# A one-core block with a 16-expert mixture: down ahead of gate and up at the last two lists, and the last list's small operations behind the row tiles

## Chip, cores and metric

The kernel runs on one core of a Trainium2 chip. The metric is the device time of one execution in microseconds (us); where several runs are named it is their median. Engines: PE multiplies matrices, DVE and ACT work elementwise, POOL does small operations and the indirect transfers, SP issues most of the plain transfers. Each engine runs its own instructions in the order in which they were written into its queue.

## The reference, cut to what matters

```python
def hier_moe(h, lp):                       # h: 512 tokens x 1024
    ...                                    # router: one group of 4, then the top 2 of its 4 experts
    y = jnp.zeros_like(h)
    for e in range(N_EXPERTS):             # 16 experts, 1024 -> 512 -> 1024
        a = jax.nn.silu(h @ lp['w_gate'][e]) * (h @ lp['w_up'][e])
        y = y + combine[..., e, None] * (a @ lp['w_down'][e])
    return y

x = x + gate1 * rmsnorm(token_mix(...), g_post_mix)
h2 = modulate(rmsnorm(x, g_pre_ffn), shift2, scale2)
x = x + gate2 * rmsnorm(hier_moe(h2, lp), g_post_ffn)
```

The parts ahead of `hier_moe` are the same in both kernels, and the change touches only what comes last.

## The kernel before

Tokens are sorted into one list per expert. The lists are worked off one after the other in the order of `SEQ`; a place in this order is a *position* n = 0 to 15, written by `position` (L1616). At each position the weights of one expert stream in from HBM: 8 loads of 512 KB for gate and up, 4 for down, issued by SP (L1305) into a ring of 25 buffers. For a full list (`heavy`, up to 128 tokens) every weight is split by ACT (L1327) and DVE (L1328) into two parts and each product is three matmuls. The short lists (`light`, 64 or 32 tokens) multiply in plain fp32 in column strips of the array. Position 13 is heavy, position 14 has 64 rows, position 15, the last, 32. Below, "list 14" is the list of position 14.

`gate_up` (L1439) multiplies by gate and up and calls hooks `mid[part]` behind each quarter; for a light list ACT then copies the sum out of PSUM (L1486). `turn_a` (L1493) transposes that (tile `at`, L1500), for a light list takes silu (ACT, L1504) and the product (DVE, L1505). `down` (L1514) multiplies by down (tiles `y0`, `y1` heavy, `yl` light), scales by the routing weight on ACT (L1555, or L1558 and L1559), and hands the rows to `release`, which POOL adds to the DRAM buffer `ybuf` with an indirect transfer (L1579, the *scatter*). Before the change, the down of position n-1 stands behind the gate and up of position n; at positions 14 and 15 it stands in the hook behind the second quarter.

The ending takes row tiles of 128 tokens. `setup` (L1819), called at position 15, issues the last weight loads, then loads of the gains (`G2`, and `G2p` for the last list), the four row tiles of x1 (`x1d`, L1830), all on SP, and on POOL an indirect gather of the last list's rows of `ybuf` (`yg`, L1838) and the four row tiles of `ybuf` (`ys`, L1841). The loads from `ybuf` can only start when the scatter of list 14 has landed. `scale(tt)` (L1848) is a square with a row sum on ACT (L1850), a scalar step on DVE (L1845), two small steps on POOL (L1846, L1855) and a product on DVE (L1852); `write(tt)` (L1857) is one DVE operation (L1859) and the store to the output (SP, L1860). The last list is not added to `ybuf`: its `yl` stays in PSUM, is added to the gathered rows (DVE, L1873), normed on its own (L1874 to L1881) and added to the output by an indirect transfer on POOL (L1887), which waits for all four stores. The order of these on each engine is that in which L1871 to L1889 are written, since `after` (L1146) ties each to the one before it on its engine.

Of the kernel before, what the change touches and what calls it, by code (L numbers as in the profile page):

```python
# [25 lines left out]
NE, DE = 16, 512  # L26
# [144 lines left out]
def bc(ap, shape):  # L171
    return ap.to_broadcast(shape)
# [5 lines left out]
def body(ctx, tc, I, C, out, dbg=None):  # L178
# [30 lines left out]
    def mm(o, l, r, start, stop):  # L209
        PE.matmul(out=o, lhsT=l, rhs=r, start=start, stop=stop)  # L210
# [92 lines left out]
    for i, nm in enumerate(("w_q", "w_k", "w_v")):  # L303
        G.dma_start(out=wst[:, 16 * i:16 * i + 16].rearrange("p (h o) -> p h o", h=4),
                    in_=I[nm].rearrange("l (h b) i o -> (l b i) h o", h=4))
    wifs = FA.get(192, "wifs")
    for i, nm in enumerate(("w_if_fwd", "w_if_bwd")):
        G.dma_start(out=wifs[:, 96 * i:96 * i + 96].rearrange("p (k j) -> p k j", k=12),
                    in_=I[nm].rearrange("l (k p) j -> p (l k) j", p=128))
# [275 lines left out]
    ybuf = dr.tile([T, D], F32, name="ybuf")  # L585
# [362 lines left out]
    for i, dst in enumerate((sh2c, s2c)):  # L948
        tp = pF("adc")
        n = 64 if i else 128  # L950
# [195 lines left out]
    def after(eng, f):  # L1146
        if eng in line and nc.cur_bb is block:
            with tc.issue_after(line[eng].ins):
                line[eng] = f()
        else:  # L1150
            line[eng] = f()
# [447 lines left out]
    def turned():  # L1599
        c, xe = fq.pop(0)  # L1600
        g = groups_of(c)
        if g > 1:
            run["nl"] += 1
            x = turn_light(xe, xtb[:, 512 * (run["nl"] % 2):512 * (run["nl"] % 2) + 512], g)
        else:
            run["nh"] += 1
            x = turn(xe, run["nh"] % 2)
        fetch_to(run["upto"])
        return x
# [6 lines left out]
    def position(n, wsrc):  # L1616
        c = SEQ[n]
        tiles = [lists_of(i) for i in ([c, NE] if c == STAR else [c])]
        pend, box = run["pend"], {}
        run["pos"] = n  # L1620
        mid = [None, None, None]
        fetch_to(run["upto"])
        if pend is not None:
            mid[0] = lambda: box.update(ya=turn_a(pend))
        if n == NE - 1:
            mid[1:] = [lambda: down(pend, box["ya"]), run["setup"]]
        xs = box["xs"] = []
        run["last"] = n == NE - 1
        ahead = lambda: xs.append(turned())
        if n + 1 < NE:  # L1630
            mid[1] = ahead
        if n == NE - 2:
            mid[1] = lambda: (ahead(), down(pend, box["ya"]))
        s_ = gate_up(tiles, wsrc, run["xs"], mid)
        if pend is not None and n < NE - 2:
            down(pend, box["ya"], mid=ahead if SEQ[n + 1] == STAR else None)
        run["pend"], run["xs"] = s_, xs
# [175 lines left out]
    fin = {}  # L1813
# [5 lines left out]
    def setup(part):  # L1819
        wsrc = run.get("wsrc")  # L1820
        if part:
            for kind, q in ((0, 3), (1, 3), (2, 0), (2, 1), (2, 2), (2, 3)):
                early[kind, q] = load(wsrc, kind, q)
                rawb.pop()
        g2 = next_raw()
        SP.dma_start(out=g2.ap, in_=bc(g2d[:, :], [128, 1024]))
        fin.update(G2=g2.ap, junk=next_raw(), ys=[next_raw() for _ in range(4)])
        fin["x1"] = [next_raw() for _ in range(4)]
        for tt in range(4):
            SP.dma_start(out=fin["x1"][tt].ap, in_=x1d[tt * 128:(tt + 1) * 128, :])  # L1830
        eng = G if part else SP
        if part:
            lb = next_raw()
            fin.update(yg=lb[:, 0:LC], G2p=lb[:, LC:2 * LC], lj=lb[:, 2 * LC:3 * LC])
            for j in range(lg_):
                m = 128 // lg_
                SP.dma_start(out=fin["G2p"][j * m:j * m + m], in_=bc(g2d[:, j * LC:j * LC + LC], [m, LC]))
            line[G] = G.indirect_dma_start(out=fin["yg"], out_offset=None, in_=parts(ybuf[:, :]), in_offset=bass.IndirectOffsetOnAxis(ap=li, axis=0),  # L1838
                                           bounds_check=T * lg_ - 1, oob_is_err=False)
        for tt in range(4):  # L1840
            line[eng] = eng.dma_start(out=fin["ys"][tt].ap, in_=ybuf[tt * 128:(tt + 1) * 128, :])  # L1841

    def inv(c):

# [25 lines left out]

    yg, lj = fin["yg"], fin["lj"]  # L1871
    sq_, tot = st[:, 24:25], psX.tile([128, 512], F32, name="tot", tag="X")
    after(V, lambda: V.scalar_tensor_tensor(yg, py, lw2, yg, op0=OP.mult, op1=OP.add))  # L1873
    after(S, lambda: S.activation(lj, yg, AF.Square, accum_out=sq_))  # L1874
    mm(tot[:, 0:1], f4, sq_, True, True)
    after(V, lambda: V.tensor_tensor(yg, yg, fin["G2p"], op=OP.mult))
    after(V, lambda: V.tensor_scalar(st[:, 26:27], tot[:, 0:1], 1.0 / D, EPS, op0=OP.mult, op1=OP.add))
    after(G, lambda: G.tensor_tensor(st[:, 25:26], st[:, 26:27], mhalf[:, 0:1], op=OP.pow))
    for tt in range(2):
        scale(tt, True)  # L1880
    after(V, lambda: V.tensor_scalar(yg, yg, st[:, 25:26], None, op0=OP.mult))  # L1881
    write(0)
    for tt in range(2, 4):
        scale(tt, True)
        write(tt - 1)
    write(3)
    after(G, lambda: G.indirect_dma_start(out=parts(outv), out_offset=bass.IndirectOffsetOnAxis(ap=li, axis=0), in_=yg, in_offset=None,  # L1887
                                          bounds_check=T * lg_ - 1, oob_is_err=False, compute_op=OP.add))
    after(S, lambda: S.mul(yob[0][:, 0:LC], py, lw2))  # L1889
# [46 lines left out]
```

## Time and profile before

| | |
|---|---|
| median of 3 runs | 633.11 us (631.62 to 636.21) |
| the profiled execution, its own time | 636.78 us |
| its span in the trace | 635.0 us |
| PE busy | 537.8 us (85%) |
| DVE, ACT, POOL busy | 352.9, 281.4, 218.8 us |
| moved by DMA | 169.27 MB, mean 267 GB/s |
| granted TensorE clock, mean | 0.94 |

The span runs from the first to the last record of the trace; 1.78 us of the execution's own time lie around it. All times below are counted from the span's start. A granted clock of 1.00 is 2.4 GHz, of 0.50 1.2 GHz.

### The profile page before, as it was taken

Reading aid. Unit: us, or ns where it says so; the run is one execution under the profiler, and the core shown is the slowest. Engines: PE = TensorE matmul, PEld = TensorE weight load, DVE = VectorE, ACT = ScalarE, POOL = GpSimd, SP = SyncE. Lnnn points to the kernel's source line nnn. Section 1 sums busy time; section 2 is a strip of 40 time slices with the busy share of each in tenths; the row PEclk is TensorE's granted clock in tenths of the full one; section 3 lists DMA queues with packets and bytes.
Section 4 is the critical chain, followed back from the end, with each engine's and each line's share of the span. In section 5 each row is a group of like instructions: output and inputs, shape, how many; then the busy total and the mean of one; then the engine's idle time right before and its main releaser. Section 6 shows DMA issues by size and latency. Waiting matters only on the chain. (4 is left out here: it accounts for less than half of the span.)

```text
span 635.0 us, 9192 instructions
## 1 busy us (share of the span) xinstructions
PE 537.8 (85%) x3097; PEld 370.3 (58%) x3097; DVE 352.9 (56%) x671; ACT 281.4 (44%) x460; POOL 218.8 (34%) x278
## 2 busy tenths in 40 slices
PE   4779989698999877999497899999999899899800
PEld 1346965587655555876286676757584545575300
DVE  3560693925336663436996989755362634673042
ACT  2560625543206243334356767546362725564130
POOL 8343850066116336816550133711312110101162
PEclk9989997899999997999798979999999999989965
DMA  9975600222399884345779799999999999999963
GB/s 265 390 265 176 257 0 6 78 62 88 110 317 290 296 345 157 118 166 199 277 263 392 253 266 392 388 344 376 398 361 386 366 389 380 382 402 389 344 223 106
DMA packets 59398, 169.27 MB, mean 267 GB/s; under 512 B 9155, under 2 KB 16835, under 8 KB 59348
## 3 DMA queue, kind: packets, MB, share of 16 engines
q1 hardware_dynamic: 51012, 156.30, 66.2%
q0 software_dynamic: 5776, 11.89, 7.2%
q10 hardware_dynamic: 2560, 0.47, 0.5%
q8 instruction: 25, 0.41, 0.3%
q14 instruction: 25, 0.20, 0.1%
HBM read 155.84 MB, written 16.73 MB: 272 GB/s over the span
## 5 line engine op out<-in xcount | busy, mean ns | idle before, releaser
L1328 DVE TENSOR_TENSOR U<-U,U 128x1024 fp32r<-128x1024 f32 x106 | 126.6, 1234 | 33.0 <-ACT U L1327 32.3
L1327 ACT CAST U<-U 128x1024 fp32r<-128x1024 f32 x106 | 107.1, 1051 | 18.1 <-PE pos L210 6.6
L210 PE MATMUL y<-U,U 128*128 128x512 f32 x352 | 93.2, 404 | 1.6 <-POOL U L213 0.6
L210 PEld LDWEIGHTS y<-U,U 128*128 128x128 f32 x352 | 64.8, 190 | 19.3 <-issue 2.0
L210 PE MATMUL gate<-U,U 128*128 128x512 f32 x166 | 50.2, 408 | 2.8 <-ACT U L1327 2.2
L210 PE MATMUL uz<-U,U 128*128 128x512 f32 x192 | 52.3, 408 | 0.2 <-ACT U L601 0.2
L210 PE MATMUL up<-U,U 128*128 128x512 f32 x164 | 49.7, 400 | 1.5 <-DVE U L1328 0.8
L213 POOL TENSOR_TENSOR U<-U,U 128x512 fp32r<-128x512 f32 (+2 forms) x32 | 42.7, 1348 | 6.5 <-ACT U L425 3.7
L210 PE MATMUL gul<-U,U 128*32 128x256 f32 (+1 forms) x368 | 44.7, 435 | 0.0
L1579 POOL DMA_INDIRECT ybuf<-U,U x8 | 13.1, 1639 | 89.6 <-ACT U L1559 63.4
L210 PEld LDWEIGHTS uz<-U,U 128*128 128x128 f32 x192 | 34.9, 189 | 11.9 <-issue 5.5
L210 PEld LDWEIGHTS gate<-U,U 128*128 128x128 f32 x166 | 31.3, 193 | 11.2 <-ACT U L1327 3.6
L1579 POOL DMA_INDIRECT ybuf<-U x8 | 14.3, 1786 | 66.4 <-ACT U L1555 38.8
L210 PEld LDWEIGHTS up<-U,U 128*128 128x128 f32 x164 | 30.9, 192 | 10.0 <-DVE U L1328 1.6
L210 PEld LDWEIGHTS gul<-U,U 128*32 128x32 f32 (+1 forms) x368 | 16.1, 116 | 18.5 <-issue 10.7
L210 PE MATMUL win<-U,U 128*128 128x512 f32 x96 | 25.6, 413 | 0.0
L1334 POOL DMA_INDIRECT U<-h2d,U x16 | 19.2, 1201 | 13.7 <-PE xlt L1346 5.5
L425 ACT CAST U<-U 128x512 fp32r<-128x512 f32 (+2 forms) x30 | 21.1, 762 | 5.7 <-DMA U<-in_w_in_dram 5.7
L213 DVE TENSOR_TENSOR U<-U,U 128x512 fp32r<-128x512 f32 (+1 forms) x18 | 15.5, 884 | 12.7 <-PE crow L210 9.0
L210 PE MATMUL yl<-U,U 128*32 128x256 f32 (+1 forms) x180 | 21.5, 438 | 0.7 <-DVE U L1505 0.7
L210 PEld LDWEIGHTS win<-U,U 128*128 128x128 f32 x96 | 18.0, 196 | 6.6 <-issue 2.5
L210 PEld LDWEIGHTS num<-U,U 128*128 128x128 f32 x128 | 17.4, 191 | 4.7 <-DVE U L920 1.7
(446 smaller groups left out, 1013.0 us busy)
## 6 DMA issues: line engine op xcount, KB each, us to landing
U<-in_w_gate_dram SPq DMA_DIRECT2D x64, 512.0 KB
U<-in_w_up_dram SPq DMA_DIRECT2D x64, 512.0 KB
U<-in_w_down_dram SPq DMA_DIRECT2D x64, 512.0 KB
U<-in_w_ada_dram SPq DMA_DIRECT2D x48, 512.0 KB
U<-in_w_in_dram SPq DMA_DIRECT2D x6, 1024.0 KB
U<-in_w_out_dram SPq DMA_DIRECT2D x4, 1024.0 KB
U<-in_x_dram SPq DMA_DIRECT2D x4, 512.0 KB
x0d<-U SPq DMA_DIRECT2D x4, 512.0 KB
```

Of the source, the lines that this page charges most:

```text
L210: PE.matmul(out=o, lhsT=l, rhs=r, start=start, stop=stop)
L213: (eng or V).tensor_tensor(o, a, b, op=OP.subtract)
L425: S.copy(hi[:, s], raw[:, s])
L1327: after(S, lambda: S.copy(hi.ap, r.ap))
L1328: after(V, lambda: V.tensor_tensor(lo.ap, r.ap, hi.ap.bitcast(F32), op=OP.subtract))
L1334: g = G.indirect_dma_start(out=xe[0:n], out_offset=None, in_=h2d[:, :], in_offset=bass.IndirectOffsetOnAxis(ap=gi[0:n], axis=0), bounds_ch ...
L1579: run["scatter"] = G.indirect_dma_start(out=to, out_offset=bass.IndirectOffsetOnAxis(ap=gi, axis=0), in_=yo[:, 0:n], in_offset=None, bound ...
```

## The change

At positions 14 and 15 the down of the list before (`turn_a` included) is called ahead of `gate_up` instead of from its hook, so its four weight loads, its matmuls and its scaling stand ahead of the gate and up of the new list. `setup` is still called behind the third quarter of position 15. In `setup` the four row tiles of `ybuf` are loaded ahead of the gather of the last list's rows. In the ending, `scale(0)` and `scale(1)` stand ahead of the last list's first operation, and its other operations stand between or behind the row tiles. Lines behind L1620 have moved by 1 to 3 in the changed file.

```diff
@@ position
-        if pend is not None:
-            mid[0] = lambda: box.update(ya=turn_a(pend))
-        if n == NE - 1:
-            mid[1:] = [lambda: down(pend, box["ya"]), run["setup"]]
         xs = box["xs"] = []
         run["last"] = n == NE - 1
         ahead = lambda: xs.append(turned())
+        if n >= NE - 2:
+
+            down(pend)
+        elif pend is not None:
+            mid[0] = lambda: box.update(ya=turn_a(pend))
         if n + 1 < NE:
             mid[1] = ahead
-        if n == NE - 2:
-            mid[1] = lambda: (ahead(), down(pend, box["ya"]))
+        else:
+            mid[2] = run["setup"]
@@ setup
+        for tt in range(4):
+            line[eng] = eng.dma_start(out=fin["ys"][tt].ap, in_=ybuf[tt * 128:(tt + 1) * 128, :])
+        if part:
             line[G] = G.indirect_dma_start(out=fin["yg"], ...)
-        for tt in range(4):
-            line[eng] = eng.dma_start(out=fin["ys"][tt].ap, in_=ybuf[tt * 128:(tt + 1) * 128, :])
@@ the ending
+    scale(0, True)
+    scale(1, True)
     after(V, lambda: V.scalar_tensor_tensor(yg, py, lw2, yg, op0=OP.mult, op1=OP.add))
+    write(0)
     after(S, lambda: S.activation(lj, yg, AF.Square, accum_out=sq_))
     mm(tot[:, 0:1], f4, sq_, True, True)
+    scale(2, True)
+    write(1)
     after(V, lambda: V.tensor_tensor(yg, yg, fin["G2p"], op=OP.mult))
     after(V, lambda: V.tensor_scalar(st[:, 26:27], tot[:, 0:1], 1.0 / D, EPS, op0=OP.mult, op1=OP.add))
+    scale(3, True)
     after(G, lambda: G.tensor_tensor(st[:, 25:26], st[:, 26:27], mhalf[:, 0:1], op=OP.pow))
-    for tt in range(2):
-        scale(tt, True)
+    write(2)
+    write(3)
     after(V, lambda: V.tensor_scalar(yg, yg, st[:, 25:26], None, op0=OP.mult))
-    write(0)
-    for tt in range(2, 4):
-        scale(tt, True)
-        write(tt - 1)
-    write(3)
```

What this does to the queues is seen at three places. The first is ACT from the scaling of list 14 (L1555) on; `gul` is the sum of gate and up of the last list, `at` its transpose, and the squares of the row tiles are the 128x1024 activations. Before:

```order
L1555 ACTIVATE U_2431<-yl,U_99 128x512
L1486 COPY U_1832<-gul 128x256
L1504 ACTIVATE U_1832<-at 128x128
L1874 ACTIVATE U_2431,U_75<-U_2431 128x256
L1850 ACTIVATE U_2431,U_75<-U_2431 128x1024
L1850 ACTIVATE U_2431,U_75<-U_2426 128x1024
L1850 ACTIVATE U_2431,U_75<-U_103 128x1024
L1850 ACTIVATE U_2431,U_75<-U_81 128x1024
```

The same stretch of ACT's queue in the changed kernel:

```order
L1555 ACTIVATE U_2431<-yl,U_99 128x512
L1852 ACTIVATE U_2431,U_75<-U_2431 128x1024
L1852 ACTIVATE U_2431,U_75<-U_2426 128x1024
L1486 COPY U_1832<-gul 128x256
L1504 ACTIVATE U_1832<-at 128x128
L1879 ACTIVATE U_2431,U_75<-U_2431 128x256
L1852 ACTIVATE U_2431,U_75<-U_103 128x1024
L1852 ACTIVATE U_2431,U_75<-U_81 128x1024
```

The squares of row tiles 0 and 1 have moved from behind the last list's operations to ahead of the copy of its `gul`; those of tiles 2 and 3 stay behind the square of its rows.

The second is PE between the transposes of list 14 and the second half of the last list's gate and up (32x256 matmuls; the 64x512 ones are the down of list 14). Before:

```order
L1500 MATMUL at<-U_81,U_1832 128x128 x4
L210 MATMUL gul<-U_2007 32x256 x2
L210 MATMUL gul<-U_2431,U_2007 32x256 x2
L210 MATMUL gul<-U_2007 32x256 x2
L210 MATMUL gul<-U_2431,U_2007 32x256 x2
L210 MATMUL gul<-U_75,U_2007 32x256 x2
L210 MATMUL gul<-U_1832,U_2007 32x256 x2
L210 MATMUL gul<-U_75,U_2007 32x256 x2
L210 MATMUL gul<-U_1832,U_2007 32x256 x2
L210 MATMUL yl<-U_2007,U_1832 64x512 x2
L210 MATMUL yl<-U_99,U_1832 64x512 x2
```

In the changed kernel:

```order
L1500 MATMUL at<-U_81,U_1832 128x128 x4
L210 MATMUL yl<-U_2007,U_1832 64x512 x2
L210 MATMUL yl<-U_2431,U_1832 64x512 x2
L210 MATMUL yl<-U_75,U_1832 64x512 x2
L210 MATMUL yl<-U_1832 64x512 x2
L210 MATMUL gul<-U_2007 32x256 x2
L210 MATMUL gul<-U_99,U_2007 32x256 x2
L210 MATMUL gul<-U_2007 32x256 x2
```

The down of list 14 has moved ahead of all of the last list's gate and up; one position earlier the heavy down of list 13 has moved ahead of all of list 14's `gul` in the same way.

The third is DVE from the last list's product (L1505) on; L1873 is the operation that adds the last `yl` to the gathered rows, L1852 the products with the gain and L1859 the sums with x1. Before:

```order
L1505 TENSOR_TENSOR U_1832<-U_1832,at 128x128
L1873 SCALAR_TENSOR_TENSOR U_2431<-yl,U_99,U_2431 128x256
L1876 TENSOR_TENSOR U_2431<-U_2431 128x256
L1877 TENSOR_SCALAR U_75<-tot 128x1
L1845 TENSOR_SCALAR U_75<-U_75 128x1
L1852 TENSOR_TENSOR U_2431<-U_2431,U_81 128x1024
L1845 TENSOR_SCALAR U_75<-U_75 128x1
L1852 TENSOR_TENSOR U_2426<-U_2426,U_81 128x1024
L1881 TENSOR_SCALAR U_2431<-U_2431,U_75 128x256
L1859 SCALAR_TENSOR_TENSOR U_2431<-U_2431,U_75,U_103 128x1024
```

In the changed kernel, where that operation is L1877, the products are L1854 and the sums L1861:

```order
L1505 TENSOR_TENSOR U_1832<-U_1832,at 128x128
L1854 TENSOR_TENSOR U_2431<-U_2431,U_81 128x1024
L1847 TENSOR_SCALAR U_75<-U_75 128x1
L1854 TENSOR_TENSOR U_2426<-U_2426,U_81 128x1024
L1877 SCALAR_TENSOR_TENSOR U_2431<-yl,U_99,U_2431 128x256
L1861 SCALAR_TENSOR_TENSOR U_2431<-U_2431,U_75,U_103 128x1024
L1847 TENSOR_SCALAR U_75<-U_75 128x1
L1854 TENSOR_TENSOR U_103<-U_103,U_81 128x1024
L1861 SCALAR_TENSOR_TENSOR U_2426<-U_2426,U_75,U_81 128x1024
L1883 TENSOR_TENSOR U_2431<-U_2431 128x256
L1884 TENSOR_SCALAR U_75<-tot 128x1
```

The products of tiles 0 and 1 have moved ahead of the operation on the last `yl`; all four sums with x1 still stand behind it.

## Rows read from the trace of the kernel before

**Rows 1.** Windows: stretch, then busy (count) per engine, granted PE clock, DMA share, GB/s

```profile
579.00:586.00 7.00, 7.00 (x29) 4.68 (x30) 3.38 (x3) 1.87 (x3) 0.00 (x0) 1.00 1.04 367
...
597.00:603.00 6.00, 3.98 (x58) 1.58 (x48) 0.29 (x1) 0.65 (x2) 1.54 (x1) 1.00 0.99 337
...
617.00:623.00 6.00, 0.00 (x0) 0.00 (x0) 5.72 (x6) 0.10 (x1) 4.24 (x4) 0.50 0.56 225
```

**Rows 2.** Timeline of POOL: start us, us, operation, [idle before, what ended it]

```profile
597.26 1.54 POOL L1579 DMA_INDIRECT ybuf<-U,U  x1 [8.48 <-ACT U L1555]
605.84 1.08 POOL L1838 DMA_INDIRECT U<-ybuf,U  x1 [7.04 <-DMA U<-g2d]
606.92 2.23 POOL L1841 DMA_DIRECT2D U<-ybuf  x4
...
626.64 1.71 POOL L1887 DMA_INDIRECT out_dram<-U,U  x1 [5.15 <-SPq L1893]
```

**Rows 3.** One line's view: issue to landing of L1579 (list 14), of L1841's first two

```profile
DMA to landing us min/median/max: 7.7/7.7/7.7
...
DMA to landing us min/median/max: 4.5/4.8/5.1
```

**Rows 4.** Timeline of DVE in the ending

```profile
610.52 0.48 DVE L1873 SCALAR_TENSOR_TENSOR U<-yl,U,U 128x256 f32<-128x256 f32 x1 [10.68 <-DMA U<-ybuf,U]
611.57 0.43 DVE L1876 TENSOR_TENSOR U<-U 128x256 f32<-128x256 f32 x1 [0.57 <-ACT U L1874]
...
612.62 0.15 DVE L1845 TENSOR_SCALAR U<-U 128x1 f32<-128x1 f32 x1 [0.24 <-ACT U L1850]
...
619.03 1.22 DVE L1852 TENSOR_TENSOR U<-U 128x1024 f32<-128x1024 f32 x1
...
621.52 1.28 DVE L1859 SCALAR_TENSOR_TENSOR U<-U,U,U 128x1024 f32<-128x1024 f32 x1
```

**Rows 5.** Timeline of PE: list 14's down, the last list

```profile
592.59 3.65 PE L210 MATMUL yl<-U,U 128*64 128x512 f32 x16
596.18 2.05 PE L210 MATMUL gul<-U,U 128*32 128x256 f32 x32
598.71 0.44 PE L1500 MATMUL at<-U,U 128*128 128x128 f32 x2 [0.47 <-ACT U L1486]
599.89 1.68 PE L210 MATMUL yl<-U,U 128*32 128x256 f32 x24 [0.75 <-DVE U L1505]
602.18 0.64 PE L210 MATMUL yl<-U 128*32 128x256 f32 x8 [0.62 <-DMA U<-in_w_down_dram]
```

**Rows 6.** Timeline of ACT in the ending

```profile
598.28 0.37 ACT L1486 COPY U<-gul 128x256 f32<-128x256 f32 x1 [1.29 <-PE gul L210]
...
611.03 0.42 ACT L1874 ACTIVATE U<-U 128x256 f32<-128x256 f32 x1 [11.52 <-DVE U L1873]
611.36 0.19 ACT L1874 ACTIVATION_READ_ACCUMULATOR U<-U 128x1 f32 x1
611.45 1.04 ACT L1850 ACTIVATE U<-U 128x1024 f32<-128x1024 f32 x1
...
612.73 1.06 ACT L1850 ACTIVATE U<-U 128x1024 f32<-128x1024 f32 x1
```

**Rows 7.** Three more windows, columns as in rows 1

```profile
555.99:559.40 3.41, 3.37 (x8) 2.69 (x9) 3.41 (x4) 3.41 (x4) 0.00 (x0) 0.50 1.03 386
...
604.00:605.00 1.00, 0.00 (x0) 0.00 (x0) 0.00 (x0) 0.00 (x0) 0.00 (x0) 1.00 0.52 190
...
607.00:608.00 1.00, 0.00 (x0) 0.00 (x0) 0.00 (x0) 0.00 (x0) 1.00 (x2) 0.59 0.40 124
```

**Rows 8.** Timeline of PE: heavy matmuls at half and at full clock

```profile
556.03 2.08 PE L210 MATMUL gate<-U,U 128*128 128x512 f32 x4 [0.53 <-DVE U L1328]
...
579.52 4.02 PE L210 MATMUL y<-U,U 128*128 128x512 f32 x17
```

**Rows 9.** Timeline of SP: down loads of list 14

```profile
573.43 4.14 SPq L1305 DMA_DIRECT2D U<-in_w_down_dram  x4
```

## The prediction

> **What bounds the kernel now.** I read the windows by stage first, then the timelines of the five engines through the last 65 us, because the chain of waits reaches back only a few microseconds from the end. The windows show two regimes [rows 1]. Up to 603 us the DMA share is 0.99 to 1.04 and PE is busy 7.00 of 7.00 us while the down of list 13 runs. From 603 us PE has nothing to do, and from 617 to 623 us DVE is busy 5.72 of 6.00 us. Between the two lies a wait for one transfer after another, and this is the stretch that the change rebuilds.
>
> The POOL timeline names that wait [rows 2, 3]. The scatter of list 14 starts at 597.26 and lands 7.7 us later, at 604.96. POOL's gather starts at 605.84, 0.88 us behind that landing; the four `ys` loads follow from 606.92, about 0.6 us apiece. The first two land 4.5 and 5.1 us after their issue, so row tile 0 is there at 611.4 and row tile 1 at 612.6. Meanwhile the last list had been finished long before: its `gul` is copied at 598.28, its `yl` begins at 599.89 and ends at 602.8 [rows 5, 6]. DVE takes it up only at 610.52, when the gather is in [rows 4]. From there the ending lasts 12.28 us on DVE: the last sum with x1 starts at 621.52 and takes 1.28 us, ending at 622.80. Store, final indirect transfer and exit follow: the trace ends 12.2 us behind that sum. In these 12.28 us nothing but DVE, ACT and the row tiles matters, and the time of the kernel moves with the end of the last sum.
>
> **The change part by part.** *Down ahead of gate and up.* No instruction is added; 24 matmuls of list 13's down and 16 of list 14's are moved, with four weight loads each past four others on SP's queue. PE is full while it happens [rows 1], so moving work within it gains little. Between list 14's transposes and its `yl` stand 16 `gul` steps today; without them `yl`, which starts at 592.59 [rows 5], starts about 0.9 us earlier. PE's switches between the two kinds of matmul become fewer, which I estimate at 0.5 us more net of the bubble that list 13's own transposes lose as cover. The scatter then starts at 595.9 instead of 597.26 and lands at 603.6. The bounds are no gain at all (PE full) and 5.0 us, the time in which SP issues four loads (4.14 us and the gap to the next) [rows 9]; I take 1.4.
>
> *Row tiles ahead of the gather.* With the same 0.88 us, the first `ys` load is issued at 604.5 instead of 606.92, the second at 605.1. The gather now stands behind them and starts near 606.9; with the 4.7 us that it took from issue to use (605.84 to 610.52) it is in at 611.6, ahead of its use below.
>
> *When row tile 1 lands.* Early bound: 605.1 plus the 5.1 us of today, 610.2. Late bound: no sooner than today, 612.6, if loads that SP issued earlier hold the DMA engines. The share is already down to 0.52 at 604 [rows 7], but tile landings grew from 4.5 to 5.1 us at that share, so at least one engine must still have been working off older loads. I take 611.6.
>
> *The squares ahead of the last list, on ACT.* This is the term that decides. ACT works in order, and the squares of row tiles 0 and 1 now stand ahead of the copy of the last list's `gul`. That copy ran at 598.28; nothing was late with it. Now it must wait for row tile 1. ACT's squares follow each other by 1.28 us (612.73 less 611.45, where tile 0's square began), so the copy starts at 611.6 + 1.28 = 612.9. From the copy to the first matmul of `yl` took 1.61 us (598.28 to 599.89) [rows 5, 6]. Behind the copy are queued the silu and all of ACT's other work; for it wait PE (transposes, `yl`), then DVE.
>
> *PE's clock.* In the ending PE's last matmul ended at 602.82, and the granted clock, 0.59 in the window 607 to 608, has fallen to half there [rows 7]. In the changed kernel PE stops about 599, behind the last `gul`, and has nothing until 613, so I take `at` and `yl` at half clock. Rows show what that means: with a granted clock of 0.50, 4 heavy matmuls took 1.88 us to the next one (0.47 each), at 1.00 17 took 4.02 us (0.24 each) [rows 7, 8]. The 32 matmuls of `yl` are of the shape that took 2.05 us for 32 [rows 5]; at half clock that is 4.1 us, and the transposes (0.44 us) and what hangs on them cost about 0.3 us more. So `yl` runs from 612.9 + 1.6 + 0.3 = 614.8 to 618.9, and DVE takes it up at 619.0, where it stood at 610.52.
>
> *What is left on DVE then.* The products of tiles 0 and 1 are done by then, hidden under `yl`. Behind the start at 619.0: 0.48; on ACT the square of the last rows, 0.42 + 0.19, then the square of tile 2 with its sum, 1.06 + 0.19, under which the first sum is hidden; then on DVE a scalar step 0.15, product 1.22, sum 1.28, the last list's 0.43 and scalar step 0.15, another 0.15, product 1.22, two sums 2.56. That is 9.5 us; DVE operations overlap by about 0.08 us at each of nine hand-overs, so 8.8 us instead of 12.28 [rows 4, 6]. The last sum ends at 627.8 instead of 622.80. The last list's final scaling comes behind it, hidden by the stores for which POOL's last transfer waits until 626.64 today [rows 2]. On SP the read of the overflow count now stands between the stores of tiles 1 and 2, which a product and a sum on DVE, 2.5 us, keep apart: no cost.
>
> Sum: 627.8 - 622.8 = **+5.0 us**. The gains, 3.5 us less on DVE and 2.4 us earlier loads, are inside this sum; the in-order wait on ACT eats more than both. Against the profiled execution's own 636.78 us this is 641.8, 0.8% more. The median of the runs shown lies 3.7 us under the profiled execution; on it the same share gives 638.1 us. One per cent, about what a measurement of this kernel can tell from no change, is 6.3 us.
>
> **The rivals.** *Row tiles land no sooner than today.* Then 612.6 replaces 611.6: +6.0 us, and up to +8 if the second half of list 14's work gains nothing and POOL's small steps wait too. For it: the share of 0.99 up to 603, and older loads still in flight. Against it: the share of 0.4 to 0.5 behind 604.
>
> *Row tiles land early, or PE's clock holds.* POOL's loads go through another queue than SP's; if an engine serves both by turns, x1's loads no longer hold them up and tile 1 lands at 610.2: +3.6 us. The Trainium skill, DMA: Bandwidth & Descriptors, section "Queues, rings and completion order", says that each DMA engine takes turns between its queues packet by packet; by that rule alone the answer would be this +3.6, and no row here shows one engine's order. With the full clock for `yl` as well it is 2.4 us less: +1.2. For the clock: nothing; PE idles longer than today.
>
> *The other side: faster.* If list 14's down really comes 5.0 us earlier, as its loads do, its scatter starts at 592.3 and lands at 600.0, tile 1 lands at 601.5 + 5.1 = 606.6, and the sum above gives 622.8, no change; with the full clock -2.4 us, and with 4.5 us to land -3.0. It decides in favour of the change from the point at which tile 1 is in before 606.6. Against it: PE full from 579 to 586, and list 14's `yl` in today's trace does not wait for its weights.
>
> *It doesn't do what it says.* List 14 comes no earlier and what ACT loses DVE gains: within 1 us of today.
>
> **How the numbers follow.** The forecast (+3.5 to +6.0 with its own bounds) gets 0.47, rows landing no sooner 0.20, rows early or clock held 0.18, faster 0.09, nothing 0.06. The predicted time is 638.1. Slower by over 1% is two thirds of the second case (0.13) and the part of the first that the spread of the runs (631.62 to 636.21) carries over 6.3 us (0.17), with 0.02 from the third: 0.32. Faster by over 1% needs the fourth case and luck: 0.03. The rest, 0.65, is within 1%. The range goes from 632.5, which leaves out most of the fourth case, to 641.5, where +8 lies.
>
> **What would show it.** Right: ACT idle for more than 10 us ahead of the square of tile 0, then two squares, then the copy of `gul`, at 611 or later; PE idle from about 599 to 613 with a granted clock of 0.50 under `yl`; DVE's operation on the last `yl` near 619, and behind it about 8.8 us to the end of the last sum. The scatter of list 14 would start near 595.9. Wrong: a copy of `gul` before 608, a `yl` of 2 us, a scatter before 594, or an ending that still takes 12 us behind the last `yl`.

## The result, and the profile after

The changed kernel takes 639.16 us (median of 15 runs, 636.54 to 641.99), the kernel before 634.01 (15 runs, 631.62 to 636.21): a ratio of 1.0084, 95% interval 1.0066 to 1.0102. It is 5.15 us slower, where +5.0 (638.1 us) was forecast.

The two profiled executions differ by only 1.7 us in span (636.7 against 635.0), because they differ ahead of the change too. The last stretch of work that stands in the same place of PE's queue in both, and in all kernels below, begins with list 12's down. Its first row in PE's timeline, in the kernel before:

```profile
568.16 2.43 PE L210 MATMUL y<-U,U 128*128 128x512 f32 x10
```

In the changed kernel the same instructions start at 564.58, so 3.58 us are added to its times when they are set beside those of before. Counted from this start, the end of the trace comes 66.84 us behind it before (635.0 - 568.16) and 72.12 after (636.7 - 564.58): +5.28 us. The end of the last sum with x1 comes 54.64 and 59.86 us behind it: +5.22.

The windows of the changed kernel, columns as in [rows 1]:

```profile
579.00:586.00 7.00, 6.29 (x31) 1.88 (x27) 0.00 (x0) 0.58 (x1) 1.54 (x1) 1.00 0.98 368
597.00:603.00 6.00, 0.00 (x0) 0.00 (x0) 0.00 (x0) 0.00 (x0) 2.27 (x4) 0.76 0.82 283
603.00:611.00 8.00, 0.46 (x2) 0.29 (x2) 0.15 (x1) 2.56 (x5) 1.85 (x3) 0.50 0.72 265
611.00:617.00 6.00, 4.10 (x35) 1.62 (x34) 3.93 (x6) 1.07 (x4) 1.65 (x2) 0.50 0.01 3
617.00:623.00 6.00, 0.36 (x2) 0.27 (x2) 5.58 (x9) 2.27 (x5) 4.33 (x4) 0.50 0.46 179
```

In the kernel before, PE was busy for 3.98 us of 597 to 603 with the end of the last list's `gul`, its transposes and its `yl` [rows 1]. That stretch is 593.4 to 599.4 here; in it PE ends `gul` at 594.88 and then has nothing. Transposes and `yl` come from 610.5 on, 4.10 us of work at a granted clock of 0.50, while the DMA engines are idle (share 0.01). They have moved behind the wait for the row tiles.

The timeline of the changed kernel, POOL, ACT, PE and DVE, answers to [rows 2, 4, 5, 6] (start us, us, operation, [idle before, what ended it]; here and below rows between those shown are left out):

```profile
564.58 2.43 PE L210 MATMUL y<-U,U 128*128 128x512 f32 x10
...
572.27 0.73 PE L210 MATMUL y<-U 128*128 128x512 f32 x2 [1.59 <-ACT U L1509]
...
587.64 2.79 PE L210 MATMUL yl<-U,U 128*64 128x512 f32 x12 [0.99 <-DVE U L1505]
...
592.30 1.54 POOL L1579 DMA_INDIRECT ybuf<-U,U  x1 [8.73 <-DMA U<-in_w_down_dram]
600.59 2.27 POOL L1840 DMA_DIRECT2D U<-ybuf  x4 [6.75 <-DMA U<-x1d]
603.16 1.08 POOL L1842 DMA_INDIRECT U<-ybuf,U  x1 [0.30 <-DMA U<-g2d]
...
607.21 1.06 ACT L1852 ACTIVATE U<-U 128x1024 f32<-128x1024 f32 x1 [15.19 <-DMA U<-ybuf]
608.39 0.15 DVE L1847 TENSOR_SCALAR U<-U 128x1 f32<-128x1 f32 x1 [20.81 <-ACT U L1852]
609.08 1.06 ACT L1852 ACTIVATE U<-U 128x1024 f32<-128x1024 f32 x1 [0.72 <-ACT U L1852]
610.14 0.35 ACT L1486 COPY U<-gul 128x256 f32<-128x256 f32 x1
610.54 0.69 PE L1500 MATMUL at<-U,U 128*128 128x128 f32 x2 [15.66 <-ACT U L1486]
611.63 0.29 DVE L1505 TENSOR_TENSOR U<-U,at 128x128 f32<-128x128 f32 x1 [3.08 <-ACT U L1504]
611.98 2.79 PE L210 MATMUL yl<-U,U 128*32 128x256 f32 x24 [0.75 <-DVE U L1505]
614.54 1.08 PE L210 MATMUL yl<-U 128*32 128x256 f32 x8
615.69 0.48 DVE L1877 SCALAR_TENSOR_TENSOR U<-yl,U,U 128x256 f32<-128x256 f32 x1 [1.44 <-PE yl L210]
...
623.16 1.28 DVE L1861 SCALAR_TENSOR_TENSOR U<-U,U,U 128x1024 f32<-128x1024 f32 x1
```

ACT waits 15.19 us for row tile 0, squares it and tile 1, and only then, at 610.14, copies the last list's `gul`, whose matmuls had ended at 594.88. PE idles for 15.66 us until the transposes. DVE's queue has the same fault: the scalar step of row tile 0 (L1847), which waits for the square, stands ahead of the last list's product (L1505). Here ACT holds the product longer, so DVE's order is not what it waits for in the end. `yl` runs from 611.98 to 615.62. From DVE's operation on it to the end of the last sum (624.44) it is 8.75 us, where [rows 4] have 12.28. The landing times of the four row tiles and of the gather:

```profile
DMA to landing us min/median/max: 6.6/8.1/9.2
...
DMA to landing us min/median/max: 8.7/8.7/8.7
```

The first two tiles took 4.5 and 5.1 us before [rows 3]; now the fastest takes 6.6.

### The profile page after: what moved, and what is told of

Read it like the earlier page. It is cut to its first block, busy times and chain, and to the rows that moved or that the text cites. A ratio compares the mean times of both kernels' runs of the same rounds, so it can differ in the third digit from the quotient of the medians.

```text
span 636.7 us, 9202 instructions
## 1 busy us (share of the span) xinstructions
PE 535.3 (84%) x3097; PEld 369.6 (58%) x3097; DVE 352.6 (55%) x671; ACT 281.5 (44%) x460; POOL 218.7 (34%) x278
## 5 line engine op out<-in xcount | busy, mean ns | idle before, releaser
L1579 POOL DMA_INDIRECT ybuf<-U,U x8 | 13.1, 1644 | 88.7 <-ACT U L1559 62.4
L210 PE MATMUL gul<-U,U 128*32 128x256 f32 (+1 forms) x372 | 43.0, 436 | 0.0
L1579 POOL DMA_INDIRECT ybuf<-U x8 | 14.5, 1808 | 65.6 <-ACT U L1555 38.8
L1500 PE MATMUL at<-U,U 128*128 128x128 f32 x58 | 10.8, 290 | 17.6 <-ACT U L1486 17.6
```

Of the source, the lines that this page charges most:

```text
L1500: PE.transpose(tp[:, q * 128:(q + 1) * 128], sg[:, q * 128:(q + 1) * 128], ident)
L1579: run["scatter"] = G.indirect_dma_start(out=to, out_offset=bass.IndirectOffsetOnAxis(ap=gi, axis=0), in_=yo[:, 0:n], in_offset=None, bound ...
```

## The experiments

All are measured beside the kernel before. "Last sum" is the end of the last sum with x1, counted from the start of list 12's down in the profiled execution, as above, with its difference to the 54.64 us of before; it is the finer measure, since a run's time moves by several us for reasons that lie ahead of this mark. The ratio is taken over the runs and isn't the quotient of the two medians.

Each "last sum" comes from one execution. Up to the scatter of list 14 it repeats well: the scatter starts 29.10 us behind the mark in the three kernels with the down in its old place (before, 2 and 7), and 27.72 to 27.76 in the change and in 1, 3, 5 and 8 to 12. Behind it the transfers differ: from the scatter to the issue of the first row tile it is 8.15 to 8.91 us in the change and in 3, 8 and 9, whose loads are alike up to there. A difference below some 0.8 us between two executions therefore shows little by itself.

| experiment | median, us | before, us | ratio, 95% interval | last sum |
|---|---|---|---|---|
| the change | 639.16 | 634.01 | 1.0084 (1.0066 to 1.0102) | 59.86, +5.22 |
| 1 down ahead alone | 635.45 | 634.95 | 1.0016 (0.9993 to 1.0039) | 54.27, -0.37 |
| 2 ending alone | 636.71 | 634.95 | 1.0034 (1.0013 to 1.0054) | 56.55, +1.91 |
| 3 squares behind the silu | 635.12 | 634.95 | 1.0001 (0.9976 to 1.0025) | 56.41, +1.77 |
| 4 clock kept, spread | 644.54 | 634.95 | 1.0148 (1.0114 to 1.0181) | 65.40, +10.76 |
| 5 as 3, x1 late | 635.27 | 634.69 | 0.9997 (0.9966 to 1.0028) | 54.37, -0.27 |
| 6 as 1, x1 late | 636.14 | 634.69 | 1.0012 (0.9983 to 1.0041) | 56.31, +1.67, of it 1.6 by PE's clock |
| 7 before, x1 late | 636.10 | 634.69 | 1.0033 (1.0002 to 1.0063) | 55.88, +1.24 |
| 8 clock kept, in order | 639.25 | 634.69 | 1.0070 (1.0041 to 1.0098) | 59.77, +5.13 |
| 9 clock kept longer | 638.84 | 634.40 | 1.0078 (1.0052 to 1.0104) | 58.83, +4.19 |
| 10 as 1, half of x1 late | 633.05 | 634.40 | 0.9980 (0.9950 to 1.0011) | 53.45, -1.19 |
| 11 as 3, mixed, half late | 632.92 | 634.40 | 0.9981 (0.9956 to 1.0006) | 52.75, -1.89 |
| 12 as 11, last list last | 630.17 | 634.92 | 0.9935 (0.9910 to 0.9959) | 52.14, -2.50 |

**Experiment 1: down ahead alone.** The changed kernel with `setup` and the ending of before.

```diff
@@ setup
-        for tt in range(4):
-            line[eng] = eng.dma_start(out=fin["ys"][tt].ap, in_=ybuf[tt * 128:(tt + 1) * 128, :])
-        if part:
             line[G] = G.indirect_dma_start(out=fin["yg"], out_offset=None, in_=parts(ybuf[:, :]),
...
+        for tt in range(4):
+            line[eng] = eng.dma_start(out=fin["ys"][tt].ap, in_=ybuf[tt * 128:(tt + 1) * 128, :])
@@ the ending
-    scale(0, True)
-    scale(1, True)
     after(V, lambda: V.scalar_tensor_tensor(yg, py, lw2, yg, op0=OP.mult, op1=OP.add))
...
```

> Only the position's part of the change (down ahead of gate and up at positions 14 and 15); the setup and the ending stand as in the kernel before. Against the kernel before (634.0 us). My theory: list 14's scatter starts 1.4 us earlier, measured from the start of the heavy down that both kernels share, and if the loads from the row buffer follow it, all behind it does too: 632.6 us, -1.4. If older loads hold the row tiles, so that they land no sooner, 634.0, no change. Rival (the loss sits here: bubbles on PE at positions 14 and 15): +3 us or more, 637 or later.

Its POOL and DVE timeline (list 12's down starts at 566.60, so 1.56 us are added):

```profile
594.34 1.54 POOL L1579 DMA_INDIRECT ybuf<-U,U  x1 [8.74 <-DMA U<-g2d]
603.36 1.08 POOL L1839 DMA_INDIRECT U<-ybuf,U  x1 [7.47 <-DMA U<-x1d]
...
608.55 0.48 DVE L1874 SCALAR_TENSOR_TENSOR U<-yl,U,U 128x256 f32<-128x256 f32 x1 [10.01 <-DMA U<-ybuf,U]
```

The scatter is 1.36 us earlier than in [rows 2] (595.90 against 597.26), the gather 0.92, and DVE's start only 0.41 (610.11 against 610.52). The gather took 5.2 us from issue to use instead of 4.7. So the step does what it says on PE, and the transfers behind it give most of it back: 0.37 us are left at the last sum, less than executions differ by, and in the runs nothing that can be told from zero. The case "no change" holds; the rival that the loss sits here falls.

**Experiment 2: ending alone.** The other half: `position` as in the kernel before.

```diff
@@ position
...
+        if n == NE - 1:
+            mid[1:] = [lambda: down(pend, box["ya"]), run["setup"]]
...
-        if n >= NE - 2:
-            down(pend)
...
```

> Only the setup's and the ending's part of the change; the down stands in its hooks as in the kernel before. My theory: ACT's copy of the last list's sum waits for the square of row tile 1, as in the changed kernel, and without the earlier scatter the loss is the changed kernel's 5.2 us and 1.4 more: 640.6 us; if older loads hold the row tiles anyway, 639.2, as late as the changed kernel. Rival (the loss sits in the positions): 634 to 636. In its trace the copy would stand behind two squares and the last yl would take 3.6 us at a granted clock of 0.50.

It fell between the two, and the trace shows that the expectation rested on a wrong queue. ACT's timeline:

```profile
593.96 0.37 ACT L1486 COPY U<-gul 128x256 f32<-128x256 f32 x1 [1.85 <-PE gul L210]
...
606.93 1.06 ACT L1851 ACTIVATE U<-U 128x1024 f32<-128x1024 f32 x1 [11.73 <-DMA U<-ybuf]
```

The copy stands ahead of the squares. `after` ties the squares to each other, but nothing ties them to the copy; which comes first is settled when the program is built, and with the down in its old place it comes out the other way round. The wait on ACT therefore belongs to neither half of the change: it arises only when both are made. What the ending costs by itself is +1.91 us: DVE's operation on `yl` starts at 611.08 + 4.88 = 615.96 instead of 610.52, as it now stands behind two products (the second ends at 610.72 in this trace) and its gather, issued behind four row tiles at 603.05, lands only 7.9 us later; 8.75 instead of 12.28 us follow. Which of the two, the order of the loads or that of the operations, costs how much was not run by itself.

**Experiment 3: squares behind the silu.** The changed kernel without the wait on ACT.

```diff
-                S.activation(a4, t4[:, :, 0:g // 2], AF.Silu)
-                V.tensor_tensor(a4, a4, t4[:, :, g // 2:g], op=OP.mult)
+                run["silu"] = S.activation(a4, t4[:, :, 0:g // 2], AF.Silu)
+                run["prod"] = V.tensor_tensor(a4, a4, t4[:, :, g // 2:g], op=OP.mult)
...
-    line.pop(V, None)
-    line.pop(S, None)
     py = down(run["pend"], keep=True)[0][:, 0:LC]
+    line[V], line[S] = run["prod"], run["silu"]
```

> The changed kernel, with ACT's first square tied behind the last list's silu and DVE's first scalar step behind its product, all else as changed. My theory: yl is done at full clock by 600 in the changed kernel's profile, so DVE's operation on it follows the product of tile 1 (square of tile 1 ends at 610.3, product at about 611.5) instead of standing at 615.69; with the same 8.75 us behind it the last sum ends at about 620.2 instead of 624.44: -4.2 us, 635.0 us, about 1 us more than the kernel before. Rival (PE or the weights of the last list are late for another reason, or the row tiles move when the copy goes early): 638 to 640, no gain.

Timeline of ACT and DVE:

```profile
595.33 0.37 ACT L1486 COPY U<-gul 128x256 f32<-128x256 f32 x1 [2.98 <-PE gul L210]
...
607.85 1.06 ACT L1852 ACTIVATE U<-U 128x1024 f32<-128x1024 f32 x1 [11.29 <-DMA U<-ybuf]
609.54 1.06 ACT L1852 ACTIVATE U<-U 128x1024 f32<-128x1024 f32 x1 [0.54 <-ACT U L1852]
612.55 0.48 DVE L1876 SCALAR_TENSOR_TENSOR U<-yl,U,U 128x256 f32<-128x256 f32 x1 [0.52 <-DMA U<-ybuf,U]
```

635.12 us against the 635.0 expected, and at the last sum 3.45 us less than the changed kernel (56.41 against 59.86). The squares ahead of the last list are thus two thirds of the loss by the last sum; by the runs, where the ratio falls from 1.0084 to 1.0001 (to 1.0025 at most), they are rather more. The edit puts the scalar step on DVE right together with the order on ACT, and the two are not separated. What is left, +1.77, is about the loss of experiment 2 (+1.91). And DVE's operation on `yl` now waits for the gather, which came 9.1 us behind its issue.

**Experiments 4, 8 and 9: PE's clock kept up.** Matmuls that nothing reads are put ahead of the last list's transposes: 60 of them, then 58 and 66 with their place in PE's queue tied.

```diff
+    wm = psX.tile([128, 512], F32, name="wm", tag="X")
+    for i in range(66):
+        with tc.issue_after(lastmm[0].ins):
+            mm(wm, ahb[:, 0:128], alb[:, 0:512], i == 0, i == 65)
+    with tc.issue_after(lastmm[0].ins):
+        py = down(run["pend"], keep=True)[0][:, 0:LC]
```

> The changed kernel, with 60 extra matmuls of 128x512 on PE, into a PSUM tile that nothing reads, between the last list's gate and up and its transposes (about 13.6 us at full clock, so PE works up to about 608.5 and waits 2 us for the copy). My theory: the transposes and the last yl run at full clock; yl then takes 2.05 us instead of 3.6, but DVE's operation on it can't start before the product of row tile 1 has ended (614.26 in the changed kernel's profile, against 615.69): -1.4 us, 637.7 us. By the prediction's own sum, which took the products as hidden, -2.0 to -2.4: 637.0. Rival (the clock isn't what makes yl long, or the wait for the square is all that counts): 639.2, no change.

This one told nothing of what the clock costs. Untied, the extra matmuls came to stand between those of lists 14 and 15, and the scatter of list 14 moved to 605.60, 37.95 us behind the mark instead of 27.72; PE's timeline shows how:

```profile
604.51 0.96 PE L210 MATMUL wm<-U,U 128*128 128x512 f32 x3
605.41 0.63 PE L210 MATMUL gul<-U 128*32 128x256 f32 x4
605.96 1.43 PE L210 MATMUL wm<-U,U 128*128 128x512 f32 x5
```

> The changed kernel, with 58 extra matmuls of 128x512 on PE into a PSUM tile that nothing reads, now tied in PE's order between the last matmul of the last list's gate and up and its transposes (13.1 us at full clock, 595 to 608 in the changed kernel's time; the transposes come at 610.5). In the fourth experiment they were spread among the matmuls from position 14 on and delayed list 14 by over 10 us. Theory: transposes and yl run at full clock, yl takes 2.05 us instead of 3.6, DVE's operation on it comes at 614.3, held by the product of row tile 1: -1.4 us against the changed kernel (0.84% over the kernel before by then, so 0.6%). Rival (the clock costs nothing): 0.84%, as the changed kernel.

Tied, but too few. The extra work ended at 611.3, the transposes came at 613.52, and the windows of PE's clock show the fall in between:

```profile
608.00:612.00 4.00, 3.33 (x15) 2.44 (x13) 0.40 (x2) 1.15 (x2) 0.16 (x1) 1.00 0.86 327
612.00:614.00 2.00, 0.48 (x2) 0.29 (x2) 1.69 (x3) 1.41 (x3) 1.92 (x2) 0.85 0.14 55
614.00:618.00 4.00, 3.25 (x33) 1.36 (x32) 0.84 (x2) 0.28 (x1) 1.29 (x3) 0.50 0.03 7
```

> The eighth experiment with 66 extra matmuls instead of 58. With 58, PE stopped 2.2 us ahead of the transposes, the granted clock fell in between (0.85 over 612 to 614, 0.50 from 614) and yl took 3.7 us as in the changed kernel. With 66, 1.8 us more, PE stops some 0.4 us ahead of them. Theory: the transposes and yl run at 1.00, yl takes 2.05 us, and DVE's operation on yl, which waited 3.76 us for PE there, comes 1.7 us earlier: 637.6 us against the eighth experiment's 639.25, 0.45% over the kernel before. Rival: yl at 0.50 once more, or as long at full clock: 0.7 to 0.8%.

With 66 the clock stays at 1.00, and `yl` takes 1.93 us (612.58 to 614.51) instead of 3.64. PE and DVE:

```profile
594.95 15.27 PE L212 MATMUL wm<-U,U 128*128 128x512 f32 x66
611.27 0.44 PE L1502 MATMUL at<-U,U 128*128 128x128 f32 x2 [1.05 <-ACT U L1488]
612.58 1.50 PE L212 MATMUL yl<-U,U 128*32 128x256 f32 x24 [0.87 <-DVE U L1507]
613.90 0.61 PE L212 MATMUL yl<-U 128*32 128x256 f32 x8
614.58 0.48 DVE L1884 SCALAR_TENSOR_TENSOR U<-yl,U,U 128x256 f32<-128x256 f32 x1 [2.06 <-PE yl L212]
```

From the square of row tile 1 (609.81) to DVE's operation on `yl` it is 4.77 us; in the changed kernel (609.08 to 615.69) and in experiment 8 (612.06 to 618.67) it is 6.61. The half clock costs 1.84 us of this chain. At the last sum 1.03 us of it is seen, since tile 1 was squared 0.8 us later in this execution (45.30 us behind list 12's down, 44.50 in the changed kernel). In the runs, 0.78% against 0.84%, it is inside the uncertainty.

**Experiments 5 to 7: x1 out of the way.** The four loads of x1, 2 MB that SP issues from about 590 on, are issued by POOL behind the row tiles and the gather: on top of experiment 3, of experiment 1 and of the kernel before.

```diff
-            SP.dma_start(out=fin["x1"][tt].ap, in_=x1d[tt * 128:(tt + 1) * 128, :])
...
+        for tt in range(4 if part else 0):
+            after(G, lambda: G.dma_start(out=fin["x1"][tt].ap, in_=x1d[tt * 128:(tt + 1) * 128, :]))
```

> The third experiment (changed kernel, squares behind the last list's silu), with the four loads of x1 taken off SP and issued by POOL behind the row tiles and the gather, so that nothing old stands in the DMA engines when the row tiles are asked for. Theory (older loads hold the row tiles): tiles 0 and 1 land 4.5 to 5 us behind their issue instead of 7.0 and 8.1 or so, their squares start 2.5 us earlier, and the ending follows as far as x1 allows: x1's first tile, issued about 605, lands by 611, and the first sum needs it at 610 to 611; 633 us, -2 against the third experiment's 635.1. Rival (the row tiles' own 2 MB set their landing): squares where they were, and x1 late by as much as it is issued later: 635 to 638.

Timeline of experiment 5, POOL, ACT and DVE:

```profile
601.56 2.24 POOL L1840 DMA_DIRECT2D U<-ybuf  x4 [6.66 <-DMA U<-g2d]
605.25 1.06 ACT L1855 ACTIVATE U<-U 128x1024 f32<-128x1024 f32 x1 [7.99 <-DMA U<-ybuf]
...
610.77 0.48 DVE L1879 SCALAR_TENSOR_TENSOR U<-yl,U,U 128x256 f32<-128x256 f32 x1 [1.71 <-DMA U<-ybuf,U]
612.15 1.29 DVE L1864 SCALAR_TENSOR_TENSOR U<-U,U,U 128x1024 f32<-128x1024 f32 x1 [0.90 <-DMA U<-x1d]
```

Row tile 0 is squared 3.7 us behind its issue (605.25 - 601.56), in experiment 3 7.1 us behind it (607.85 - 600.78). The queues tell why. In the changed kernel, from the issue of the row tiles to the square of tile 0 (600.6 to 607.2; queue, packets, MB, share of 16 engines):

```profile
q0 software_dynamic: 428, 1.59, 69.0%
q1 hardware_dynamic: 236, 0.54, 21.0%
```

In experiment 5, over the same stretch of work (601.6 to 605.25):

```profile
q0 software_dynamic: 210, 0.79, 61.8%
q1 hardware_dynamic: 13, 0.01, 0.7%
```

SP's queue still moved 0.54 MB of older loads beside the row tiles (0.68 MB in experiment 3, from 600.78 to 607.85); without x1 it moved 0.01. That the older loads hold the row tiles is shown. But part of the gain is spent at once: DVE waits 1.71 us for the gather and 0.90 for x1. The last sum comes 2.04 us earlier than in experiment 3, as expected; the runs (ratio 0.9997 against 1.0001) don't show it, and 2 us, 0.3%, is about what their intervals leave open.

> The first experiment (down ahead alone, setup and ending as before), with the four loads of x1 issued by POOL behind the gather and the row tiles. Theory (older loads ate the 1.4 us by which the scatter came earlier): the gather takes 4.5 us or less from issue to use instead of 5.2, the ending starts 0.7 to 1.4 us earlier, 634.4 us against the first experiment's 635.45; x1's first tile, issued about 607, lands by 613, just when the first sum wants it. Rival (x1 late costs more than it frees): 636 to 638.

The gather came 2.85 us behind its issue (5.2 in experiment 1), but the first sum waits for x1. The +1.67 us at the last sum are not the price of that: in this execution PE's granted clock fell to 0.50 (window 578 to 580) during the down of list 13, the 17 matmuls that took 4.15 us in experiment 1 took 5.77, and the scatter started 1.6 us late, 29.35 us behind the mark instead of 27.74.

```profile
576.41 5.77 PE L210 MATMUL y<-U,U 128*128 128x512 f32 x17
...
616.87 1.28 DVE L1863 SCALAR_TENSOR_TENSOR U<-U,U,U 128x1024 f32<-128x1024 f32 x1 [3.47 <-DMA U<-x1d]
```

Counted from the scatter, the last sum ends after 26.96 us, in experiment 1 after 26.53 (620.87 - 594.34). So the earlier gather brings nothing at the end, and the expected gain of 1.05 us is missed. The rival, that x1 late costs more than it frees, isn't shown either: 0.43 us is less than executions differ by, and 636.14 us lies in its range only beside a kernel before of 634.69, a ratio of 1.0012 that can't be told from 1.

> The kernel before, with the four loads of x1 issued by POOL behind the gather and the row tiles. It tells what that step brings by itself, without the down ahead. Theory: the share of the DMA engines was already down to 0.4 to 0.5 when its gather was issued, so little is freed: -0.5 us, 634.4; x1's first tile, issued about 609.5, lands at 615, when the first sum stands at 615.4. Rival (x1 late): 636 to 638.

The same by itself, in the kernel before: DVE waits 1.77 us for x1 (the first sum starts at 614.02), the last sum is 1.24 us late, and the runs agree (1.0033, at least 1.0002); here the rival holds.

**Experiments 10 to 12: loads in the order of their use.** Tiles 0 and 1 of x1 stay on SP, 2 and 3 go behind the rows. Experiment 10 does this on experiment 1. Experiment 11 does it on experiment 3, and POOL issues row tiles 0 and 1, then the gather, then row tiles 2 and 3. Experiment 12 is 11 with the last list's operations behind all four row tiles.

```diff
@@ experiment 12, the ending, against the changed kernel
     scale(0, True)
     scale(1, True)
-    after(V, lambda: V.scalar_tensor_tensor(yg, py, lw2, yg, op0=OP.mult, op1=OP.add))
     write(0)
-    after(S, lambda: S.activation(lj, yg, AF.Square, accum_out=sq_))
-    mm(tot[:, 0:1], f4, sq_, True, True)
     scale(2, True)
...
     write(3)
+    after(V, lambda: V.scalar_tensor_tensor(yg, py, lw2, yg, op0=OP.mult, op1=OP.add))
+    after(S, lambda: S.activation(lj, yg, AF.Square, accum_out=sq_))
+    mm(tot[:, 0:1], f4, sq_, True, True)
...
```

> The first experiment (down ahead alone) with the loads of x1's tiles 2 and 3 issued by POOL behind gather and row tiles, tiles 0 and 1 left on SP. In the sixth experiment, with all four late, the gather was in 2.85 us behind its issue instead of 5.2, but the first sum waited 3.47 us for x1. Theory (the row tiles are held by what is still to be loaded, so the loads should be put in the order of their use): the gather is in 3.5 to 4 us behind its issue, no sum waits for x1, and the last sum ends about 1.3 us earlier, measured from list 12's down, than in the kernel before: 633.5 us against 634.7. Rival (the 2 MB of x1 and the 2 MB of rows take their time in any order): 634.7 to 636.

The last sum comes 1.19 us earlier than before, 1.3 expected; the gather is in 3.5 us behind its issue and no sum waits for x1. The runs (633.05, ratio 0.9980) agree, but their interval holds 1.

> The third experiment (changed kernel, squares behind the last list's silu), POOL's order changed to row tiles 0 and 1, gather, row tiles 2 and 3, then x1's tiles 2 and 3; x1's tiles 0 and 1 stay on SP. Theory: tile 0 is squared 4.2 us behind its issue (7.0 in the third experiment, 3.7 in the fifth), the gather is in before the second product ends, DVE is busy from then to the last sum, which ends some 1.7 us earlier, from list 12's down, than in the kernel before: 633.0 us. Rival: the gather or x1 is late by what the rows gain: 634.7 to 636.

-1.89 us at the last sum, 1.7 expected; tile 0 is squared 4.4 us behind its issue. The interval of the runs just holds 1.

> The eleventh experiment with the last list's operations behind all four row tiles: squares of tiles 0 to 3 on ACT, four products and four sums on DVE, and only then the operation on yl, its square, sum, step, product and scaling. Theory (from tile 0 on DVE is the bound, and behind the last sum POOL's last transfer waits 3.85 us for the stores anyway): DVE loses from the path 0.40 of the operation on yl, 0.33 and 0.07 of the product and the scalar step, and the 0.42 us that it waited for the square of tile 2 behind the last list's square: -1.2 us against the eleventh experiment, the last sum 51.5 us behind the start of list 12's down against 54.64 in the kernel before (-3.1); the last list's chain takes about 3.0 us behind the last sum and is done before the stores have landed. About 631.5 us against 634.5, ratio 0.995. Rival (the last list's chain becomes the end): the last transfer on POOL starts later than 3.85 us behind the last sum, ratio 0.997 to 0.999.

The end of experiment 12, DVE and POOL (list 12's down starts at 563.55):

```profile
614.41 1.28 DVE L1867 SCALAR_TENSOR_TENSOR U<-U,U,U 128x1024 f32<-128x1024 f32 x1
615.62 0.48 DVE L1888 SCALAR_TENSOR_TENSOR U<-yl,U,U 128x256 f32<-128x256 f32 x1
616.67 0.42 DVE L1891 TENSOR_TENSOR U<-U 128x256 f32<-128x256 f32 x1 [0.58 <-ACT U L1889]
617.31 0.16 DVE L1892 TENSOR_SCALAR U<-tot 128x1 f32<-128x1 f32 x1 [0.22 <-PE tot L210]
618.13 0.35 DVE L1894 TENSOR_SCALAR U<-U,U 128x256 f32<-128x256 f32 x1 [0.66 <-POOL U L1893]
...
619.57 1.70 POOL L1895 DMA_INDIRECT out_dram<-U,U  x1 [1.47 <-DVEq L1901]
```

The last list's whole chain is done 2.8 us behind the last sum (618.48 - 615.69), while POOL's last transfer starts 3.88 us behind it, as it did in experiment 11 (3.85). The work costs nothing there. The last sum came 0.6 us earlier than in experiment 11, not 1.2: tile 0 was squared 4.9 us behind its issue this time, 0.5 more. By their ratio the runs lie 0.65% under the kernel before (interval 0.41 to 0.90, 2.6 to 5.7 us), and 630.17 us is the fastest of all. The profiled executions show 2.50 us of this at the last sum and 2.2 at the end of the trace; where the rest comes from stays open.

## Why the prediction was right

The mechanism was the one forecast, the in-order wait on ACT; the sum came out as closely as it did partly by luck, as two of its terms were off and others made up for them. Step by step, with 3.58 us added to the changed kernel's times:

| step | predicted | measured |
|---|---|---|
| scatter of list 14 | 595.9 | 595.88 |
| its landing takes | 7.7 | 7.6 |
| first row tile asked for | 604.5 | 604.17 |
| row tile 1 there, its square starts | 611.6 | 612.66 |
| copy of the last `gul` | 612.9 | 613.72 |
| `yl` | 614.8 to 618.9 | 615.56 to 619.20 |
| DVE takes up `yl` | 619.0 | 619.27 |
| from there to the end of the last sum | 8.8 | 8.75 |
| end of the last sum | 627.8 | 628.02 |
| sum against before | +5.0 | +5.22 (runs +5.15) |

*The squares ahead of the last list, on ACT.* "This is the term that decides": it did. Taking only this order away, on ACT and DVE (experiment 3), returns 3.45 of the 5.22 us, though the row tiles land no earlier.

*When row tile 1 lands* was the weakest term and it missed by 1.06 us, although the loads were asked for 0.33 us earlier than taken, to the value of the rival "row tiles land no sooner than today" (612.6). The cause is the one named there for the late bound, older loads of SP: experiment 5 takes them away, and tile 0 lands in about half the time. Smaller errors pay for most of it: the copy followed the last square by its own 1.06 us instead of 1.28, and `yl` took 3.64 us instead of 4.1 at half clock. The right sum thus holds one cancellation.

*Row tiles ahead of the gather* has a step that failed without being seen. The gather was to take the 4.7 us of [rows 2, 4] and be in at 611.6. Behind four row tiles it took 8.7 us and was in at 603.16 + 8.7 + 3.58 = 615.44. The late `yl` covered that; in experiment 3, where it doesn't, DVE waits for the gather. So "the gains ... are inside this sum" was too kind: without the wait on ACT the change would not gain 3.5 and 2.4 us, it still loses 1.8 at the last sum, and in the runs it gains nothing (1.0001).

*Down ahead of gate and up* brought the 1.4 us at the scatter (1.36 in experiment 1), of which 0.4 reach the end: the transfers behind it slow down by the rest. The sum had 0.9 for the `gul` steps and 0.5 for switches net of a bubble; no row gave the 0.5, and the runs show only the total. The bubbles are in the timeline above: 1.59 us at the start of list 13's down and 0.99 ahead of list 14's `yl`, both for transposes and elementwise work that other matmuls covered before.

*PE's clock.* 2.05 us and 0.3 were put on it; experiment 9 shows 1.84 on the chain.

*What the runs can tell.* The prediction took 1% as about the smallest change to be told from none. With 15 runs each the interval is 0.36% wide, and the 0.84% is clear of it.

The rival on early rows drew on the Trainium skill, DMA: Bandwidth & Descriptors, section "Queues, rings and completion order", by which each DMA engine takes turns between its queues packet by packet. The rival made of it that x1's loads don't hold the row tiles up and that tile 1 is there at 610.2. The queue rows agree with the page in that both queues moved data in the same stretch (1.59 and 0.54 MB); they differ from what the rival made of it, since tile 0 took 7.1 us with the older loads (experiment 3) and 3.7 without. What the rival put at nothing is the share that the other queue takes: in the first 3.65 us behind the issue of tile 0 POOL's queue moved 0.60 MB beside 0.49 MB of SP's in the changed kernel, and 0.79 beside 0.01 in experiment 5. In what order one engine served the two is in no view here.

The side that forecast a faster kernel needed list 14's down 5.0 us earlier; it came 1.4 earlier.

## What to carry to other kernels

Where engines work in order, read the queue, not the diff: an operation that waits for a late transfer must not stand ahead of one whose input is long there, and two edits that leave a queue in order apart can put it there together. A load issued earlier need not land earlier while older loads of other queues are still moving: row tile 0 was asked for 2.75 us earlier than before and landed 0.6 us earlier, tile 1 no earlier at all. Here it paid to issue the loads in the order in which their data is used. Small operations that only a last transfer needs cost nothing behind the last long one, under a wait that was there anyway (experiment 12).

## What was not expected of the hardware

- Up to list 12's down the kernels run the same program, and yet this point lay between 563.28 us (experiment 2) and 568.16 (before) in the profiled executions. That is more than most effects studied here; counting from a common mark made them readable. Behind the mark, too, one execution (experiment 6) lost 1.6 us to a fall of PE's granted clock that its twins didn't show; comparing the start of the scatter tells it from an effect of the edit.
- The landing of a 512 KB row tile depended on what another queue still had to move: 3.7 us beside 0.01 MB (experiment 5), 6.6 beside 0.54 MB (the changed kernel), 7.1 beside 0.68 MB (experiment 3). The gather took 2.85, 4.7, 5.2 or 9.1 us from issue to use, depending on what stood beside and ahead of it.
- PE at half clock costs a stretch of 32 short matmuls 1.7 us (3.64 against 1.93). In experiment 8, where the extra work ended at 611.3 and the transposes came at 613.52, the granted clock was 0.85 over 612 to 614 and 0.50 behind; in experiment 9, where it ended at 610.2 and they came at 611.27, it stayed at 1.00.
